# A hybrid backbone on one core: modulation gathered by 32x32 block transposes, tokens loaded first, bias rows without a second buffer

## The chip, the cores and the metric

The kernel runs on one core of one Trainium2 chip. The metric is device time in microseconds (us). The core has a matrix engine (TensorE, PE in the profile), a vector engine (VectorE, DVE), a scalar engine (ScalarE, ACT), a general one (GpSimd, POOL) and a sync engine (SyncE, SP) that here only issues DMA transfers. Each executes its own instructions in order, and the DMA issues of one queue go out in order as well. On chip, tiles lie over 128 partitions; a "128x1024" tile has 1024 numbers in each.

## The reference

256 latent tokens and 256 context tokens of width 2048 pass through two layers. All data are fp32. Layer 0 mixes with a gated DeltaNet (bidirectional, in chunks of 64 tokens) beside neighbourhood attention, layer 1 with a short convolution, and each layer ends in a SwiGLU network with 5632 hidden units. Every layer is modulated by six rows (shift, scale and gate, twice) that are products of one conditioning vector with a 2048 x 12288 matrix. In short:

```python
def modulate(x, g, shift, scale):
    return rmsnorm(x, g) * (1 + scale[..., None, :]) + shift[..., None, :]

for l in range(DEPTH):                                     # DEPTH = 2
    sh1, sc1, g1, sh2, sc2, g2 = split(silu(c) @ ada_w[l] + ada_b[l], 6)
    h = modulate(x_lat, norm_mix[l], sh1, sc1)
    if l % 2 == 0:
        csh1, csc1, ... = split(silu(c_ctx) @ ada_w[l] + ada_b[l], 6)
        hc = modulate(x_ctx, norm_mix[l], csh1, csc1)
        y = even_mixer(h, hc, ...)     # [DeltaNet * silu(za) | attention] @ w_out
    else:
        y = shortconv_mixer(h, ...)
    x_lat = x_lat + g1 * y
    x_lat = x_lat + g2 * swiglu(modulate(x_lat, norm_ffn[l], sh2, sc2), ...)
return rmsnorm(x_lat, final_norm)
```

In the DeltaNet each chunk needs the inverse of a unit triangular 64x64 matrix. In the attention each head adds to its scores a bias from a table of 15 x 31 numbers and a banded mask over the columns of the token grid.

## The kernel before

Nearly all time goes into products of the tokens with large fp32 weights. A weight tile of 128x1024 is loaded raw (512 KB, one issue on the SP queue, L229); ScalarE copies its high part into `whi` (L172), VectorE subtracts to get the low part `wlo` (L243), and PE adds three products for each output tile: high by high, high by low, low by high. `tm_stream` (L274 to L304; matmuls L291, L292, L294) gives outputs with tokens on partitions, `fm_stream` (L306 to L325; matmuls L317 and L321) outputs with features on partitions. Each stream is a Python generator; `drive` advances it one weight tile at a time and runs other work between. The written order is the program's wish. A scheduler with a model of the engines' times then sets the order on each engine and queue, so code that is moved by one step can come out many instructions away.

The start: the modulation of the first mixer is computed eight blocks at a time. `start_block(b)` (L524) loads 4 MB of `ada_w` in four tiles `araw0` (each of two DMAs) and multiplies them with the conditioning vectors (L533, 16 matmuls of 512 columns). `start_tokens(b, ...)` (L537) copies the sums to `mrow` (L540), picks columns by eight matmuls (L546), forms shift and scale, transposes two 128-wide pieces of the normalised tokens `xn` (L191) and writes the modulated tiles `modt` and their high and low parts (L560 to L562). `token_stats` (L565) loads the 4 MB of `xn` (L569), sums squares on ScalarE (L573), takes the root, scales `xn` on VectorE (L576), and is called once, behind `start_block(0)`. The first two streams (`s0`, `s1`) run beside blocks 1 to 7.

Later modulation: for layer 0's remaining parts `ada_mixer` keeps a running sum with one VectorE instruction per half tile (L389) beside the streams and closes a block with four column sums (L396). `ada_job` (L335 to L364) serves layer 1 and the last gate of layer 0: seven jobs of two blocks each. A block adds 16 products (L346) of 128x1024 into `acc`, and then the 128 partitions must be added up and the 1024 sums turned into eight columns of 128. Three of the jobs are of kind "row" (their result goes to DRAM), four of kind "sh" or "sc" (shift and scale).

The middle: after the context's part come the projections QB (two streams of 16 steps), then KB, VB, KB, VB. `plan` calls the inverses (`inverses`, L939) when the count of steps reaches the numbers of `P_INV`: two for the context, then two for the latents. An inverse multiplies by the diagonal blocks `xd` and `xdT`, which SP loads before it; L962, L969 and L975 are its products, and its first product stands behind the latest stream matmul (`issue_after(last_mm[0])`). Then `scan` (L982) and the latents' recurrence follow in pieces between the streams ZA and w_out.

Attention runs head by head with one head ahead: `na_scores` (L1172) loads the head's bias rows `br` (two DMAs, one buffer), its keys `kb` and queries `qb`, adds the band into `bq` (L1183), and takes scores and softmax; `na_values` (L1199) does the rest. The gate `za` is computed by a `tm_stream` whose `za_evac` (L1215) applies silu, multiplies by the norm's gain and stores 128x512 to DRAM on the SP queue (L1220). Its staging tile `zst` has two buffers (`NST`). Then w_out's weights come through a pool of six raw buffers.

## Time and profile before

| | us |
|---|---|
| median of 3 runs | 2819.64 |
| lowest and highest | 2818.58, 2827.38 |
| the profiled execution's own time | 2823.79 |
| its span in the trace | 2822.0 |
| mean granted clock | 0.989 |
| PE busy | 2719.8 (96%) |
| DVE busy | 1920.1 (68%) |
| ACT busy | 1301.9 (46%) |

The span runs from the first recorded instruction to the last, and 1.8 us of the execution's own time lie outside it. A busy PE is the union of matmuls in flight. The granted clock is a share of PE's full speed, so a stretch with 0.86 ran part of the time at the lower of the two levels.

### The profile page before, as it was taken

The page shows a single profiled execution, that of the slowest core. Times are in us where ns is not written, and L with a number is a line of the kernel's source. Part 1 is how long each engine was busy: PE and PEld are TensorE (multiplying, and loading weights), DVE is VectorE, ACT ScalarE, POOL GpSimd, SP SyncE. Part 2 cuts the span into 40 slices and gives each one's busy share as a digit, 9 for nine tenths or more (in the row PEclk, how much of TensorE's full clock was granted, in tenths as well). Part 3 has the DMA queues.
Part 4 walks back from the last instruction along what each step waited for, and adds up shares of the span by engine and source line. Part 5 has one row for each costly group of instructions (what it writes and reads, how often), then busy time and mean ns, then how long its engine had stood idle before and what let it go on. Part 6 is the DMA issues. An engine that isn't in the chain of part 4 may idle for free.

```text
span 2822.0 us, 40405 instructions
## 1 busy us (share of the span) xinstructions
PE 2719.8 (96%) x15113; PEld 2277.5 (81%) x15113; DVE 1920.1 (68%) x2647; ACT 1301.9 (46%) x1943; POOL 50.3 (2%) x77
## 2 busy tenths in 40 slices
PE   5999989999999999999999999999999999999998
PEld 3799989887778788888888878878878888888886
DVE  2377768866767888776678667797678644445665
ACT  2267534322454544444455555444454444444554
POOL 0000100000000000000000000000000000000000
PEclk9999999999999999999999999999999999999999
DMA  9945578887758699987788647998559766656663
GB/s 342 325 135 157 148 234 259 270 250 226 213 200 285 208 333 340 345 291 255 264 283 286 197 154 275 333 327 286 186 196 326 247 193 186 187 188 215 190 192 126
DMA packets 286399, 680.78 MB, mean 241 GB/s; under 512 B 57209, under 2 KB 100833, under 8 KB 284795
## 3 DMA queue, kind: packets, MB, share of 16 engines
q1 hardware_dynamic: 281828, 668.73, 71.3%
q10 hardware_dynamic: 4375, 9.48, 0.9%
q8 instruction: 118, 1.93, 0.3%
q14 instruction: 78, 0.64, 0.1%
HBM read 657.63 MB, written 20.48 MB: 240 GB/s over the span
## 4 chain that ended last, share of the span: by engine, by line
PE 78%; DMA 10%; DVE 6%; ACT 3%; issue 2%; SPq 1%; DVEq 0%; POOL 0%; ACTq 0%
PE mm L294 19%; PE mm L291 19%; PE mm L292 19%; PE mm L321 7%; DMA araw<-in_ada_w_dram 5%; PE mm L300 2%; PE mm L301 2%; PE mm L302 2%; DVE wlo L243 2%; PE sm L191 2%; DMA raw<-in_od_w_in_dram 1%; PE sm L533 1%; DVE acc L346 1%; DVE acc L389 1%; PE gd L321 1%
## 5 line engine op out<-in xcount | busy, mean ns | idle before, releaser
L243 DVE TENSOR_TENSOR wlo<-raw,whi 128x1024 fp32r<-128x1024 f32 x800 | 971.1, 1222 | 436.8 <-ACT whi L172 430.9
L172 ACT ACTIVATE whi<-raw 128x1024 fp32r<-128x1024 f32 x800 | 842.2, 1059 | 825.6 <-PE mm L294 618.9
L292 PE MATMUL mm<-wlo,fhi 128*128 128x512 f32 x1232 | 472.4, 392 | 0.0
L291 PE MATMUL mm<-whi,fhi 128*128 128x512 f32 x1232 | 470.7, 396 | 0.0
L294 PE MATMUL mm<-whi,flo 128*128 128x512 f32 x1232 | 392.2, 392 | 0.1
L346 DVE SCALAR_TENSOR_TENSOR acc<-araw,cT,acc 128x1024 f32<-128x1024 f32 x224 | 287.3, 1283 | 130.2 <-DMA araw<-in_ada_w_dram 123.5
L294 PEld LDWEIGHTS mm<-whi,flo 128*128 128x128 f32 x1232 | 230.8, 188 | 51.1 <-DVE flo L1288 0.5
L292 PEld LDWEIGHTS mm<-wlo,fhi 128*128 128x128 f32 x1232 | 231.8, 188 | 48.7
L291 PEld LDWEIGHTS mm<-whi,fhi 128*128 128x128 f32 x1232 | 231.9, 188 | 48.2
L291 PE MATMUL mm<-whi,ahi 128*128 128x512 f32 x672 | 259.8, 392 | 0.0
L292 PE MATMUL mm<-wlo,ahi 128*128 128x512 f32 x672 | 259.3, 391 | 0.0
L294 PE MATMUL mm<-whi,alo 128*128 128x512 f32 x672 | 209.8, 392 | 0.0
L321 PE MATMUL mm<-hllo,whi 128*128 128x256 f32 x608 | 172.9, 289 | 0.0
L321 PE MATMUL mm<-hlhi,whi 128*128 128x256 f32 x570 | 161.7, 292 | 2.2 <-DVE hlhi L561 1.9
L175 ACT ACTIVATE ahi<-prodT 128x256 fp32r<-128x256 f32 x176 | 73.2, 417 | 194.6 <-PE mm L292 183.9
L389 DVE SCALAR_TENSOR_TENSOR acc<-araw,cT,acc 128x512 f32<-128x512 f32 x192 | 142.7, 747 | 29.1 <-DMA araw<-in_ada_w_dram 27.3
L321 PE MATMUL mm<-hlhi,wlo 128*128 128x256 f32 x570 | 157.8, 289 | 0.0
L292 PEld LDWEIGHTS mm<-wlo,ahi 128*128 128x128 f32 x672 | 126.2, 188 | 27.7
L294 PEld LDWEIGHTS mm<-whi,alo 128*128 128x128 f32 x672 | 126.1, 188 | 27.3
L291 PEld LDWEIGHTS mm<-whi,ahi 128*128 128x128 f32 x672 | 126.2, 188 | 27.1
L292 PE MATMUL mm<-wlo,dhi 128*128 128x512 f32 x336 | 126.4, 396 | 2.2 <-DVE wlo L243 2.2
L291 PE MATMUL mm<-whi,dhi 128*128 128x512 f32 x336 | 123.8, 397 | 0.6 <-DVE u_t L1428 0.6
(419 smaller groups left out, 4194.0 us busy)
## 6 DMA issues: line engine op xcount, KB each, us to landing
araw<-in_ada_w_dram SPq DMA_DIRECT2D x288, 512.0 KB
raw<-in_ffn_w_down_dram SPq DMA_DIRECT2D x176, 512.0 KB
raw<-in_ffn_w_gate_dram SPq DMA_DIRECT2D x160, 512.0 KB
raw<-in_ffn_w_up_dram SPq DMA_DIRECT2D x160, 512.0 KB
raw<-in_ev_w_in_dram SPq DMA_DIRECT2D x112, 512.0 KB
araw<-in_ada_w_dram SPq DMA_DIRECT2D x192, 256.0 KB
raw<-in_od_w_in_dram SPq DMA_DIRECT2D x96, 512.0 KB
raw<-in_ev_w_out_dram SPq DMA_DIRECT2D x32, 512.0 KB
```

What stands on the lines that cost most here:

```text
L172: ACT.activation(dst, src, AF.Copy)
L175: ACT.activation(hi, src, AF.Copy)
L191: return PE.transpose(dst, src, ident[:n, :n])
L243: last_lo[0] = DVE.tensor_tensor(lo, raw, hi, op=OP.subtract).ins
L291: PE.matmul(ps[ti][n], a, hi[:, n * 512:(n + 1) * 512], start=first, stop=False)
L292: PE.matmul(ps[ti][n], a, lo[:, n * 512:(n + 1) * 512], start=False, stop=False)
L294: last_mm[0] = PE.matmul(ps[ti][n], b, hi[:, n * 512:(n + 1) * 512], start=False, stop=False).ins
L300: PE.matmul(ps[ti][n], lh(t), hi[:, c_], start=False, stop=False)
L301: PE.matmul(ps[ti][n], lh(t), lo[:, c_], start=False, stop=False)
L321: last_mm[0] = PE.matmul(ps[f][:, n * 256:(n + 1) * 256], wt, mv(w, k), start=False, stop=i == len(ks) - 1 and g == len(group) - 1 and j = ...
L346: DVE.scalar_tensor_tensor(acc, raw, cT[:, k:k + 1], acc, op0=OP.mult, op1=OP.add)
L389: DVE.scalar_tensor_tensor(accs[n], raws.pop(i), cT[:, k:k + 1], accs[n], op0=OP.mult, op1=OP.add)
```

## The change

Five things change. First, in `ada_job` the gather of a block is replaced by `sum_parts`: VectorE transposes `acc` in blocks of 32x32 (128x1024 in one instruction), adds up each group of 32 (to 128x32), and four fp32 matmuls with the 128x32 constant `fold` add the four groups of partitions. Their result has features on partitions, so "sh" and "sc" jobs take it as it is, and "row" jobs copy it, transpose it once (8 rows of 128) and go on as before. The split of `acc` (ACT and VectorE), 16 selection matmuls, and for "sh" and "sc" a copy and a transpose go away. Second, `token_stats()` is called ahead of `start_block(0)`. Third, the bias rows are loaded straight into `bq`, which has three buffers now, and the band is added in place; `br` is gone. Fourth, the gate store goes out on GpSimd's queue. Fifth, `P_INV` counts differ.

```diff
-P_INV = (30, 32, 79, 80)
+P_INV = (32, 34, 81, 82)
...
+    def sum_parts(dst, pool_, acc, n, tag, bufs):
+        at = pool_.tile([128, 4 * n, 32], F32, name="accT", tag=tag, bufs=bufs)
+        ar = pool_.tile([128, n, 4], F32, name="accR", tag="accR", bufs=bufs)
+        DVE.transpose(at.rearrange("p b r -> p (b r)"), acc)
+        DVE.tensor_reduce(ar.rearrange("p k b -> p (k b)"), at, axis=AX.X, op=OP.add)
+        for b in range(4):
+            PE.matmul(dst[b * 32:b * 32 + 32, 0:n], C("fold"), ar[:, :, b], start=True, stop=True)
...
-            split(ah, al, acc, DVE)
-            for f in range(8):
-                for a in (ah, al):
-                    PE.matmul(p[0:8, 0:128], pick[:, 7 - f:15 - f], a[:, f * 128:(f + 1) * 128],
-                              start=f == 0 and a is ah, stop=f == 7 and a is al)
-            g = pool_.tile([16, 128], F32, name="grow", tag="grow", bufs=1)[0:8]
-            acopy(g, p[0:8, 0:128])
+            sum_parts(p, pool_, acc, 8, "accT", 1)
             if kind == "row":
+                gc = pool_.tile([128, 8], F32, name="gcol8", tag="gcol8", bufs=1)
+                acopy(gc, p[:, 0:8])
+                pc = smt()
+                transpose(pc[0:8, 0:128], gc)
+                g = pool_.tile([16, 128], F32, name="grow", tag="grow", bufs=1)[0:8]
+                acopy(g, pc[0:8, 0:128])
                 ACT.dma_start(row_d[l, seg][fs_], g)
                 continue
-            pc = smt()
-            transpose(pc[:, 0:8], g)
-            ada_done(l, seg, kind, gamma, fs_, pc[:, 0:8])
+            ada_done(l, seg, kind, gamma, fs_, p[:, 0:8])
...
+    token_stats()
     sums = start_block(0)
-    token_stats()
...
-        bq = nap.tile([128, 6, 64], F32, name="bq", tag="bq", bufs=2)
-        br = nap.tile([128, 6, 64], F32, name="br", tag="br", bufs=1)
+        bq = nap.tile([128, 6, 64], F32, name="bq", tag="bq", bufs=3)
...
-            SP.dma_start(br[half * 64:half * 64 + 64], src)
+            SP.dma_start(bq[half * 64:half * 64 + 64], src)
...
-        DVE.tensor_tensor(bq, br, bandf[:, None, :].to_broadcast([128, 6, 64]), op=OP.add)
+        DVE.tensor_tensor(bq, bq, bandf[:, None, :].to_broadcast([128, 6, 64]), op=OP.add)
...
-        SP.dma_start(zd[:, ti, n * 512:(n + 1) * 512], o)
+        POOL.dma_start(zd[:, ti, n * 512:(n + 1) * 512], o)
```

Added lines shift the numbers behind them by 5 or 6: L962, L969 and L975 become L968, L975 and L981, L396 becomes L402, L1180 becomes L1185, and L1220 becomes L1225.

PE's order at the first inverse, before. `mm` are the sums of the QB stream (L321, with `hlhi` and `hllo` the latents' high and low parts), `gd` those of the inverse, and L396 sums a modulation block of layer 0:

```order
L321 MATMUL mm<-hllo,whi 128x256
L321 MATMUL mm<-hlhi,wlo 128x256
L962 MATMUL gd<-xd,n_3970 32x32 x32
L396 MATMUL sm<-cs,acc 128x1 x4
L969 MATMUL gd<-xdT,Y 32x32 x32
L975 MATMUL gd<-Y,xdT 32x32 x32
L321 MATMUL mm<-hlhi,whi 128x256
L321 MATMUL mm<-hllo,whi 128x256
L321 MATMUL mm<-hlhi,whi 128x256
```

The same place in the changed program, where L317 with `h_100` is the first matmul of the KB stream:

```order
L321 MATMUL mm<-hllo,whi 128x256
L321 MATMUL mm<-hlhi,wlo 128x256
L968 MATMUL gd<-xd,n_3970 32x32 x32
L317 MATMUL mm<-h_100,whi 128x512
L321 MATMUL mm<-hllo,whi 128x256
L321 MATMUL mm<-hclo,whi 128x256
L321 MATMUL mm<-h_100,wlo 128x256 x2
L317 MATMUL mm<-h_100,whi 128x512
L321 MATMUL mm<-hllo,whi 128x256
```

The inverse's first product now stands behind the last matmul of QB, with no other work between; the column sums (L402 now) stand 24 rows of QB's matmuls earlier, and L975 and L981, the inverse's next products, follow 22 rows after the first one, among KB's matmuls.

SP's queue where the first attention heads load, before (`vb_d` and `nst` are the last value stores of VB, `kb`, `qb` and `vb` a head's loads):

```order
L1142 DMA vb_d<-nst 128x512 x2
L1180 DMA br<-in_ev_rpb_dram 64x6x64 x2
L1181 DMA kb<-kb_d 128x512
L1142 DMA vb_d<-nst 128x512
L1182 DMA qb<-qb_d 128x256
L1181 DMA kb<-kb_d 128x512
L1182 DMA qb<-qb_d 128x256
L1202 DMA vb<-vb_d 128x4x128
L1180 DMA br<-in_ev_rpb_dram 64x6x64 x2
L1202 DMA vb<-vb_d 128x4x128
```

And in the changed program:

```order
L1148 DMA vb_d<-nst 128x512 x3
L1185 DMA bq<-in_ev_rpb_dram 64x6x64 x2
L1148 DMA vb_d<-nst 128x512
L1186 DMA kb<-kb_d 128x512
L1187 DMA qb<-qb_d 128x256
L1185 DMA bq<-in_ev_rpb_dram 64x6x64 x2
L1186 DMA kb<-kb_d 128x512
L1187 DMA qb<-qb_d 128x256
L1207 DMA vb<-vb_d 128x4x128
L1185 DMA bq<-in_ev_rpb_dram 64x6x64 x2
L1207 DMA vb<-vb_d 128x4x128
```

The second head's bias rows stand right behind the first head's keys and queries, where before the first head's loads and the second's keys stood between, and the third head's rows come one place earlier.

SP's queue at the gate stores, before:

```order
L1220 DMA zd<-zst 128x512 x2
L1202 DMA vb<-vb_d 128x4x128
L1220 DMA zd<-zst 128x512
L229 DMA raw<-in_ev_w_out_dram 128x1024 x2
L1181 DMA kb<-kb_d 128x512
L1182 DMA qb<-qb_d 128x256
L229 DMA raw<-in_ev_w_out_dram 128x1024
```

And in the changed program, where `raw` are the weights of w_out and `araw` those of the modulation:

```order
L1185 DMA bq<-in_ev_rpb_dram 64x6x64 x2
L390 DMA araw<-in_ada_w_dram 128x512 x2
L229 DMA raw<-in_ev_w_out_dram 128x1024 x6
L1207 DMA vb<-vb_d 128x4x128
L229 DMA raw<-in_ev_w_out_dram 128x1024
L390 DMA araw<-in_ada_w_dram 128x512
```

Six weight tiles now stand in a row and no store `zd` is on this queue. The four stores stand on GpSimd's queue, one behind the other, with only fills of `acc` around them.

## Rows read from the trace of the kernel before

**Rows 1.** The line of busy time by engine (first part of the page): busy us, share of the span, instructions.

```profile
PE 2719.8 (96%) x15113; PEld 2277.5 (81%) x15113; DVE 1920.1 (68%) x2647; ACT 1301.9 (46%) x1943; POOL 50.3 (2%) x77
```

**Rows 2.** Table of busy time by stretch: the stretch, its length, then busy us and instructions of PE, PEld, DVE, ACT and POOL, the granted clock, the DMA share, and GB/s. The first two rows are the start and the first weight stream, then come five stretches round two inverses, the bias rows and the gate store, the latents, and all that follows.

```profile
0.00:45.40 45.40, 17.31 (x68) 5.15 (x68) 13.41 (x29) 17.91 (x22) 1.74 (x7) 1.00 0.96 336
45.40:150.00 104.60, 102.74 (x818) 78.19 (x815) 34.80 (x91) 22.74 (x36) 0.00 (x0) 1.00 0.95 305
404.00:428.00 24.00, 20.66 (x351) 20.07 (x349) 12.39 (x18) 8.67 (x14) 0.52 (x1) 0.86 0.83 225
600.00:624.00 24.00, 17.93 (x307) 15.61 (x306) 13.56 (x20) 5.57 (x10) 0.00 (x0) 0.86 0.87 299
684.00:708.00 24.00, 18.23 (x73) 13.06 (x72) 12.33 (x18) 6.02 (x10) 0.00 (x0) 0.86 0.74 207
770.00:780.00 10.00, 6.99 (x51) 6.42 (x49) 7.98 (x18) 6.51 (x12) 0.00 (x0) 1.00 0.87 232
806.00:840.00 34.00, 27.88 (x158) 22.74 (x157) 20.45 (x66) 19.07 (x68) 0.21 (x1) 0.90 0.15 48
924.00:2810.00 1886.00, 1868.13 (x8440) 1529.13 (x8440) 1296.70 (x1440) 899.65 (x1151) 13.94 (x16) 1.00 0.73 245
```

**Rows 3.** The chain of waits in the first 46 us: start, length, what held the chain.

```profile
16.99 13.91 DMA xn<-in_ctx_dram
...
41.86 3.64 PE sm L533 x16
```

**Rows 4.** Timeline of the start, three engines together in this order: the last eight conditioning products of block 0 and its selection matmuls (PE), the scaling of the tokens and the low parts of three weight tiles (DVE), the third high part and the four modulated tiles (ACT), the first stream matmuls, and the first half of block 1's products (PE). Columns: start, length, engine, line, operation, count, and in brackets the idle time before and what ended it.

```profile
21.26 1.94 PE L533 MATMUL sm<-araw,cT 128*32 128x512 f32 x8 [1.15 <-DMA araw<-in_ada_w_dram]
...
24.00 1.87 PE L546 MATMUL sm<-cs,mrow 128*128 128x2 f32 x8 [0.80 <-DVE mrow L540]
...
35.34 4.87 DVE L576 TENSOR_SCALAR xn<-xn,n0r 128x2048 f32<-128x2048 f32 x4
...
40.13 3.49 DVE L243 TENSOR_TENSOR wlo<-raw,whi 128x1024 fp32r<-128x1024 f32 x3
...
38.13 1.06 ACT L172 ACTIVATE whi<-raw 128x1024 fp32r<-128x1024 f32 x1 [0.29 <-DMA raw<-in_ev_w_in_dram]
...
40.78 1.93 ACT L560 ACTIVATE modt<-sm,sh,sc 128x256 f32<-128x256 f32 x4 [1.59 <-PE sm L191]
...
45.43 2.08 PE L317 MATMUL mm<-h,whi 128*128 128x512 f32 x4
...
49.73 1.06 PE L533 MATMUL sm<-araw,cT 128*32 128x512 f32 x8
```

**Rows 5.** What the gather costs today, and the nearest rows to what replaces it: one of the 16 selection matmuls of a block and the stream matmul behind them (timeline), 64 small fp32 records of an inverse and the eight records of four column sums of layer 0 (timeline, 0.75 and 1.02 us from first start to last end), the vector engine's low part of the accumulator and its 32x32 transpose of 32x128 (by line and form: min/median/max ns), and a stretch in which a gather falls (columns as in the table by stretch).

```profile
1028.86 0.22 PE L355 MATMUL sm<-ah,pick 128*8 128x128 f32 x1
...
1029.82 0.45 PE L292 MATMUL mm<-wlo,fhi 128*128 128x512 f32 x1
...
415.26 0.75 PE L962 MATMUL gd<-xd,n 32*32 32x32 f32 x64
...
415.98 1.02 PE L396 MATMUL sm<-cs,acc 128*128 128x1 f32 x8
...
L176 DVE TENSOR_TENSOR al<-acc,ah x14: 1214/1224/1226, 1018.5 to 2311.1; 128x1024 fp32r<-128x1024 f32 x14
...
L880 DVE STREAM_TRANSPOSE dgs<-nt x32: 292/302/309, 223.3 to 501.5; 32x128 f32<-32x128 f32 x32
...
1850.00:1910.00 60.00, 57.07 (x272) 45.35 (x270) 53.40 (x64) 27.09 (x36) 0.96 (x1) 1.00 0.95 345
```

**Rows 6.** The first bias rows: the DMA issue of the second head's rows (SPq is the sync engine's queue), the addition that waits for them, and the two matmuls that stand behind it (timeline).

```profile
686.62 1.27 SPq L1180 DMA_DIRECT2D br<-in_ev_rpb_dram  x2
...
696.13 0.56 DVE L1183 TENSOR_TENSOR bq<-br,cs 128x384 f32<-128x384 f32 x1 [5.74 <-DMA br<-in_ev_rpb_dram]
...
697.88 0.50 PE L292 MATMUL mm<-wlo,hlhi 128*128 128x512 f32 x1 [2.27 <-DVE wlo L243]
...
701.60 2.08 PE L838 MATMUL gd<-cs,gm 128*128 128x128 f32 x8 [2.99 <-DVE AT L1074]
```

**Rows 7.** The gate stores: two issues on the sync queue, then one, then the first two weight tiles of w_out; the first matmul that needs such a tile (timeline); and, by line and form, the vector engine's tensor_scalar of 128x512.

```profile
760.08 1.69 SPq L1220 DMA_DIRECT2D zd<-zst  x2
...
769.51 0.32 SPq L1220 DMA_DIRECT2D zd<-zst  x1
...
769.88 0.92 SPq L229 DMA_DIRECT2D raw<-in_ev_w_out_dram  x2
...
776.41 1.20 PE L291 MATMUL mm<-whi,yhi 128*128 128x512 f32 x4 [3.01 <-ACT whi L172]
...
L1196 DVE TENSOR_SCALAR s<-s,l x16: 435/480/488, 709.0 to 831.8; 128x512 f32<-128x512 f32 x16
```

**Rows 8.** At the first inverse: the four raw weight issues after the loads of the diagonal blocks, and the scalar engine's first high part from them (timeline); and the modulation sums of layer 0 (costliest groups of the page: count, busy us, mean ns, idle before).

```profile
415.20 2.21 SPq L229 DMA_DIRECT2D raw<-in_ev_w_in_dram  x4
...
420.81 1.06 ACT L172 ACTIVATE whi<-raw 128x1024 fp32r<-128x1024 f32 x1 [4.37 <-DMA raw<-in_ev_w_in_dram]
...
L389 DVE SCALAR_TENSOR_TENSOR acc<-araw,cT,acc 128x512 f32<-128x512 f32 x192 | 142.7, 747 | 29.1 <-DMA araw<-in_ada_w_dram 27.3
```

**Rows 9.** The third inverse's first 64x64 product, and a value product at the end of the latents' chain (timeline of PE).

```profile
616.29 0.44 PE L962 MATMUL gd<-xd,n 64*64 64x64 f32 x2 [4.13 <-DVE xd L977]
...
830.66 3.78 PE L1211 MATMUL gd<-PT,vb 128*128 128x256 f32 x8 [3.66 <-ACT PT L167]
```

2 lines of the change are left out of this document (removed).

## The prediction

> **What bounds the kernel now.** I read the busy times by engine first: PE is busy 96% of the span [rows 1], so time comes back only where PE does less, waits less or runs at a higher clock. The table by stretch shows where that can be. From 924 us on PE is idle 17.9 of 1886 us and the clock is full [rows 2], so two thirds of the run have almost no waits to remove. The idle time sits in the start (28.1 of 45.4 us), at the two inverses (3.3 us of 404 to 428, 6.1 us of 600 to 624), at the first bias rows (5.8 us of 684 to 708), at w_out's first weights (3.0 us of 770 to 780) and in the latents (6.1 us of 806 to 840) [rows 2]. [...] A stretch at 0.86 does 24 x 0.14 = 3.4 us less work than at 1.00. So a wait is worth its idle time and, where it takes the clock down, up to 3.4 us on top. Then I read the chain of waits at the start and the timelines at the places that the change touches.
>
> **The start.** The chain runs through the tokens' DMA, which holds it from 16.99 for 13.91 us, and ends in L533 x16 of 3.64 us [rows 3]. Behind the last tokens stand the scaling on DVE (35.34 to 40.21), three low parts (40.13 to 43.62), the four modulated tiles on ACT, and the first stream matmul at 45.43 [rows 4]. In the changed program the same 8.4 MB (tokens and block 0) go out in the other order. The DMA engines are 0.96 busy over the start [rows 2], so the last byte still lands at about 30.9 (16.99 + 13.91). But what lands last is then block 0, and the tokens' sums, root and scaling are done in its shadow. Behind it stand: the last eight of L533 1.94, `mrow` 0.7 to 0.8 (L546's idle before it), L546 1.87 [rows 4], shift and scale (three short operations, for which I allow 0.6), and two of the low parts (1.2 each) that DVE takes before them. That puts the modulated tiles at about 30.9 + 1.9 + 0.8 + 1.9 + 0.6 + 1.2 = 37.3 or earlier, against 40.78, and the first stream matmul 3.5 us or so before 45.43. What is late next is the weights: from 45 to 150 us the DMA share is 0.95 at 305 GB/s [rows 2], and a part of the gain can be lost again to a later block's data. L533 of block 1 (two halves of 1.06 at full speed, against 3.64 for 16 at the start) moves behind the stream's start in place of standing ahead of it. I take -3.5, from -6 (all of that and a cheaper L533) to -1.
>
> **The gather.** PE's 16 selection matmuls take 0.96 us a block (1028.86 to 1029.82), and there are 14 blocks, as the 14 low parts show [rows 5]: 13.4 us, beside nothing, since PE is the bound there. Four fp32 fold matmuls come in their place, each recorded as two: eight records. The nearest rows are 64 records in 0.75 us with weights of 32 columns and eight in 1.02 us with weights of 128 [rows 5], so 0.09 to 1.02 a block. The fold has a weight of 128x32 and eight columns out; its loads have all partitions as L396's do, and I take 0.70. That is (0.70 - 0.96) x 14 = -3.6. For "row" blocks a transpose is added, for the others one goes: nothing. ACT loses a copy of 1024 columns a block and was not waited for. DVE loses `al` (1.22) and gains a transpose and a reduction of the same 1024 numbers, which no row shows at this size: between 1.22 each (the row of `al`, same length) and 2.4 (eight times the transpose of 128 numbers, 302 ns). I take 1.24 each, near the row of the same length, so +1.26 us a block on DVE. From 924 us on DVE is busy 1296.7 of 1886 us [rows 2], which hides it. The cover is thin at one place, 1850 to 1910, where DVE is busy 53.4 of 60 and PE already idle 2.9 [rows 5]: two blocks, half a microsecond each, +1 (0 to +5, at 2.4 each). Sum -2.6.
>
> The row of `al` has 1224 ns for 1024 numbers, and the transpose's 302 ns for 128 is more than an eighth of it [rows 5]. [...]
>
> **Bias rows.** DVE, in order, waits 5.74 us at 696.13 for `br`; the issue of such rows is at 686.62, since the single buffer comes free only with the addition of the head before [rows 6]. Behind the waiting addition stand the low part and the mask product, and PE waits 2.27 us at 697.88 and 2.99 us at 701.60 for them [rows 6]; with the clock (0.86) the place costs 5.3 + 3.4 = 8.6 us. With three buffers SP can issue the rows two heads ahead, and the second head's stand behind the first head's keys. The adding itself stays at 0.56. What is late next is the weights' high part and the latents' scores; the clock need not come back whole. I take -6 (0 to -8.6).
>
> **w_out's first weights.** The sync queue issues two gate stores at 760.08 and one at 769.51, each of which must wait for `za_evac`, and the first two raw tiles of w_out stand behind it at 769.88; PE waits 3.01 us at 776.41 for the high part [rows 7]. Off this queue, the tiles go out as their buffers come free. I take -2 (0 to -3).
>
> **First inverse.** SP's issues of the KB weights at 415.20 come behind the loads of the diagonal blocks, and the high part waits 4.37 us for them and starts at 420.81 [rows 8]. PE fills 0.75 + 1.02 us of that with L962 and L396, and something over a microsecond with L969 and L975, standing idle 3.3 us. In the changed order L402 stands 24 rows ahead and L975 and L981 22 rows behind: the weights' wait is filled by L968 alone, so about 1.2 us more idle, and DVE must do five modulation sums (0.75 each [rows 8]) before the copies of `xd` where it had one. I take +3 (-2 to +6).
>
> **Third inverse.** PE waits 4.13 us at 616.29 for `xd` from DVE [rows 9]. The new step number moves the call by two steps, the chain through DVE is the same, and nothing in the order takes the sums out of its way: 0 (-9.4, if the 6.1 idle and the 3.4 of clock both go, to +5).
>
> **Latents' end.** The last recurrence has stream work to hide behind: before its first state product some 105 matmuls of ZA and 51 of w_out are left, in the changed order 43 and 51. At 1868.13/8440 = 0.22 us a record [rows 2] that is 14 us less cover. The tail, 806 to 840, has 6.1 us idle and a clock of 0.90, with waits like the 3.66 us at 830.66 for ACT [rows 2, 9]. I take +1.5 (0 to +8), since the chain also starts earlier by what the bias rows and w_out give.
>
> **Sum.** -3.5 - 2.6 - 6 - 2 + 3 + 0 + 1.5 = -9.6 us, against the profiled execution's 2823.79 (a span of 2822.0 and 1.8 around it): 2814.2. That execution lies 4.2 above the median of 2819.64; medians are compared, so I take the difference from there: 2810.0.
>
> **The rivals.**
> Smaller gain: the DMA queue, 0.95 busy until 150 us, takes back the start's 3.5, and the first inverse costs its upper 6: 2810 + 3.5 + 3 = 2816.5. For it: no block's bytes become fewer. Against it: the tokens' work does leave the chain.
> Faster: the third inverse meets its `xd` in time because two more steps of stream lie ahead of it: 2810 - 9.4 = 2800.6. Against it: the wait is on DVE's queue, which moves with it.
> Slower, by one mechanism: the latents' recurrence runs out of cover. If the 14 us that left are uncovered in full, and the clock falls twice at 3.4, the place costs 20.8 in place of 1.5: 2829.3. It decides from about 11 us of uncovered chain on, where the whole gain is used up. For it: the tail has idle time already. Against it: most of the recurrence waits on itself while PE does attention, not only streams.
> The gather waits: the folds stand in PE's order right behind a chain of two DVE operations (2.5 us); if 0.8 us of that shows in each of 14 blocks, 2810 + 11.2 = 2821.2.
> Stores late on GpSimd: `zst` has two buffers, and between the pair and the third store lie 9.4 us [rows 7]; a store would have to be some 8 us late for the evacuation to wait. Then about +4: 2814. DVE is busy with tensor_scalar work of 480 ns beside them [rows 7]. [...]
>
> **How the numbers follow.** Forecast 0.50 (own range 2803 to 2817), smaller gain 0.25, faster 0.10, latents 0.08, the gather waits 0.04, stores late 0.03. 0.3% is 8.5 us, which is about what a measurement of this kernel can tell from no change: faster is under 2811.2, slower over 2828.1. Faster: two thirds of the forecast (0.33), all of the faster case, a quarter of the smaller gain, a little of the last: 0.50. Slower: most of the latents' case and the tails of the others, 0.08. The rest, 0.42, is within. The range 2798 to 2822 leaves out the latents' case and the outer edges of the others.
>
> **What would show it.** Right: first L317 at 41 to 43 us; eight fold records within 0.7 us of each other; no wait for the bias rows at 690 to 705 and a clock near 1.00 there; w_out's high part without the 3 us wait; DVE transposes near 1.2 us. Wrong: the stream's gain gone by 150 us, PE idle in front of the folds, a longer idle time in the latents' tail, or waits at the first or third inverse other than told.

## The result and the profile after

The changed kernel takes 2837.34 us (median of 6 runs, 2835.21 to 2839.90) against 2825.08 for the kernel before (6 runs, 2818.58 to 2828.20): a ratio of 1.0047, 95% interval 1.0035 to 1.0059. It is slower by 12 to 13 us, where the forecast was 10 us faster. (The forecast started from 2819.64, the median of the first three runs; three more put it at 2825.08.) The profiled execution took 2837.88 us, its span is 2836.1.

The line of busy time by engine, which answers to [rows 1]:

```profile
PE 2720.1 (96%) x14999; PEld 2268.8 (80%) x14999; DVE 1934.5 (68%) x2661; ACT 1284.1 (45%) x1924; POOL 58.2 (2%) x81
```

PE is busy for the same 2720 us in a span that is 14 us longer, though 114 matmuls fewer are recorded. The table by stretch, same stretches and columns as [rows 2]:

```profile
0.00:45.40 45.40, 19.27 (x85) 9.71 (x86) 13.35 (x29) 17.79 (x22) 0.73 (x5) 1.00 0.96 326
45.40:150.00 104.60, 100.02 (x777) 72.23 (x777) 32.71 (x82) 21.10 (x33) 0.99 (x2) 0.98 0.97 309
404.00:428.00 24.00, 16.38 (x128) 16.30 (x128) 9.99 (x12) 6.89 (x7) 0.52 (x1) 0.86 0.82 223
600.00:624.00 24.00, 21.86 (x161) 20.48 (x159) 12.22 (x19) 4.10 (x5) 2.41 (x3) 1.00 0.76 190
684.00:708.00 24.00, 21.59 (x103) 16.59 (x102) 19.26 (x30) 7.72 (x14) 0.00 (x0) 1.00 0.92 277
770.00:780.00 10.00, 6.99 (x28) 5.88 (x29) 7.89 (x13) 8.73 (x20) 1.08 (x2) 0.69 0.49 169
806.00:840.00 34.00, 29.22 (x187) 24.04 (x185) 17.87 (x54) 16.95 (x72) 0.00 (x0) 1.00 0.15 48
924.00:2810.00 1886.00, 1863.82 (x8320) 1517.92 (x8319) 1311.82 (x1454) 886.27 (x1135) 13.94 (x16) 0.99 0.73 247
```

Some places look as the forecast wanted them: PE idle 2.4 us in 684 to 708 (5.8 before) and 2.1 in 600 to 624 (6.1), with the clock at 1.00 in both where it was 0.86. (The second stretch no longer holds the third inverse, which has moved behind it, as the rows below show.) Others are worse: 404 to 428 has 7.6 us idle (3.3 before), and 770 to 780 has the clock at 0.69. Time per stretch doesn't yet tell what a wait is worth; fixed points of the program do. The timelines of PE have these points at the following times (starts of instructions, ends where it says so; "value product" is the attention's L1211, L1216 after; the first down projection is counted up to the first matmul of the next product, the last one from the end of the matmul before it):

| | before | after |
|---|---|---|
| first stream matmul (L317) | 45.4 | 38.9 |
| eighth block's selection matmuls (L546, L552) | 146.5 | 149.0 |
| QB's last first-tile matmul (L317), then KB's first | 400.6, 428.1 | 402.5, 431.8 |
| latents' first state product | 719.2 | 738.2 |
| end of the ZA stream | 768.5 | 759.3 |
| last value product | 837.0 | 849.1 |
| end of w_out | 922.3 | 934.3 |
| first down projection, length | 254.0 | 256.5 |
| last down projection, length | 242.6 | 246.3 |
| end of the last stream | 2808.3 | 2822.1 |

PE's rows of the start, which answer to [rows 4] (the first conditioning products, which by the row now follow the tokens' statistics, the first stream matmul, the eighth selection), and the wait for weights that stood beside the first inverse ([rows 8]) and now stands bare (the matmul that waits is one of QB's last, so these are QB's weights and not yet KB's, as I had read them):

```profile
23.01 1.94 PE L539 MATMUL sm<-araw,cT 128*32 128x512 f32 x8 [10.78 <-DVE n0s L219]
...
38.94 2.08 PE L317 MATMUL mm<-h,whi 128*128 128x512 f32 x4 [0.57 <-DVE h L567]
...
149.04 0.50 PE L552 MATMUL sm<-cs,mrow 128*128 128x2 f32 x4
```

```profile
425.48 0.58 PE L321 MATMUL mm<-hlhi,whi 128*128 128x256 f32 x1 [7.62 <-ACT whi L172]
```

The start is 6.5 us ahead at 39 and 2.5 behind at 149. The ZA stream ends 9.2 us earlier, and yet w_out ends 12 later. From the last value product to the end of w_out it is 85 us in both. So this product, and the chain that leads to it, sets the end of the middle, and not the ZA stream beside it. It is 12.1 of the 14.1 us. The rest lies behind: the down projections are 2.5 and 3.7 us longer, although no line of theirs was changed, and the other stretches behind w_out, where the gathers fall, are about 4 us shorter.

PE's timeline of the chain, before and then after: the first product of the latents' first inverse (the third inverse), the latents' first state product and the last value product:

```profile
602.00 0.75 PE L962 MATMUL gd<-xd,n 32*32 32x32 f32 x64
...
719.19 1.05 PE L1000 MATMUL gd<-state,kT 128*128 128x128 f32 x8
...
836.98 1.97 PE L1211 MATMUL sm<-PT,vb 128*128 128x256 f32 x8 [0.31 <-issue]
```

```profile
628.99 0.75 PE L968 MATMUL gd<-xd,n 32*32 32x32 f32 x64
...
738.24 1.05 PE L1006 MATMUL gd<-state,kT 128*128 128x128 f32 x8
...
849.10 1.97 PE L1216 MATMUL sm<-PT,vb 128*128 128x256 f32 x8 [0.39 <-issue]
```

The third inverse starts 27 us late, the recurrence 19 us, and its end is 12 us late. Between start and end of the recurrence stands another wait. Timelines of the changed kernel round the gate stores, in the order of their causes: SP's issue of the six w_out tiles, the vector engine's addition of bias rows, the first three gate stores on GpSimd, the scalar engine's third gate evacuation, the vector engine behind it, and PE behind that:

```profile
752.79 8.51 SPq L229 DMA_DIRECT2D raw<-in_ev_w_out_dram  x6
...
758.67 0.56 DVE L1188 TENSOR_TENSOR bq<-bq,cs 128x384 f32<-128x384 f32 x1 [4.59 <-DMA bq<-in_ev_rpb_dram]
...
761.17 0.67 POOL L1225 DMA_DIRECT2D zd<-zst  x1 [88.84 <-DVE zst L1224]
...
762.97 0.54 POOL L1225 DMA_DIRECT2D zd<-zst  x1 [1.13 <-DVE zst L1224]
...
772.21 0.54 POOL L1225 DMA_DIRECT2D zd<-zst  x1 [8.70 <-DVE zst L1224]
...
770.60 0.60 ACT L1222 ACTIVATE zst<-mm 128x512 f32<-128x512 f32 x1 [13.38 <-DMA zd<-zst]
...
771.23 0.69 DVE L1224 TENSOR_TENSOR zst<-zst,gnb 128x512 f32<-128x512 f32 x1 [8.57 <-ACT zst L1222]
...
773.01 2.08 PE L1026 MATMUL gd<-R,xdT 128*128 128x128 f32 x8 [7.32 <-DVE R L1009]
```

Three megabytes of weights go out from 752.79 on. The first evacuations were done by 757, but the gain's multiplication on DVE stands behind the addition, which waits 4.59 us for its rows; so the stores start at 761. Then the first of them needs until 770.5 to land, `zst` has two buffers, and ACT waits 13.38 us, DVE 8.57 and PE 7.32. PE's wait of 3.01 us for w_out's weights [rows 7] is gone; this one is for `R`, a tile of the recurrence.

The list of DMA issues gives the median time from issue to landing (last column, us), for the first two stores and then for the other two, ahead of which no weights had been issued for 11 us:

```profile
zd<-zst POOLq DMA_DIRECT2D x2, 256.0 KB, 9.0
...
zd<-zst POOLq DMA_DIRECT2D x2, 256.0 KB, 2.4
```

The same queue thus took 9.0 us with six weight tiles issued ahead of it and 2.4 without them.

### The profile page after: what moved, and what is told of

Read it like the earlier page. It is cut to its first block, busy times and chain, and to the rows that moved or that the text cites. A ratio compares the mean times of both kernels' runs of the same rounds, so it can differ in the third digit from the quotient of the medians.

```text
span 2836.1 us, 40147 instructions
## 1 busy us (share of the span) xinstructions
PE 2720.1 (96%) x14999; PEld 2268.8 (80%) x14999; DVE 1934.5 (68%) x2661; ACT 1284.1 (45%) x1924; POOL 58.2 (2%) x81
## 5 line engine op out<-in xcount | busy, mean ns | idle before, releaser
L172 ACT ACTIVATE whi<-raw 128x1024 fp32r<-128x1024 f32 x800 | 842.9, 1059 | 907.0 <-PE mm L294 627.5
L321 PE MATMUL mm<-hllo,whi 128*128 128x256 f32 x608 | 173.0, 289 | 0.0
L321 PE MATMUL mm<-hlhi,whi 128*128 128x256 f32 x570 | 161.8, 292 | 10.6 <-ACT whi L172 7.6
L321 PE MATMUL mm<-hlhi,wlo 128*128 128x256 f32 x570 | 159.2, 290 | 0.0
L176 DVE TENSOR_TENSOR alo<-prodT,ahi 128x256 fp32r<-128x256 f32 x176 | 74.3, 424 | 85.5 <-PE mm L294 80.0
```

The costliest lines, as they stand in the source:

```text
L172: ACT.activation(dst, src, AF.Copy)
L176: (eng or DVE).tensor_tensor(lo, src, hi, op=OP.subtract)
L321: last_mm[0] = PE.matmul(ps[f][:, n * 256:(n + 1) * 256], wt, mv(w, k), start=False, stop=i == len(ks) - 1 and g == len(group) - 1 and j = ...
```

## The experiments

Two theories were put up first. **A, the late recurrence:** the inverses called two steps later start the recurrence 19 us later, and its end is passed on. **B, the gate stores:** the wait of 13.38 us is passed on. Times are medians; ratios are to the kernel before as it was timed beside each run, with their 95% interval.

**Undoing the step numbers, the gate store's queue, both, or giving a third buffer.** All four start from the changed kernel:

```diff
-P_INV = (32, 34, 81, 82)          # first and third run
+P_INV = (30, 32, 79, 80)
...
-        POOL.dma_start(zd[:, ti, n * 512:(n + 1) * 512], o)     # second and third
+        SP.dma_start(zd[:, ti, n * 512:(n + 1) * 512], o)
...
-NST = 2                            # fourth
+NST = 3
```

> The changed kernel with the old step numbers for the inverses. Its trace has the latents' first state product at 738.2 us (before: 719.2) and the recurrence's last value product at 849.1 (before: 837.0). Theory A (late latents: the inverses called two steps later start the recurrence 19 us later, and its end sets the end of w_out): the first state product comes back to about 719, and the time falls by 10 to 14 us, to 2823 to 2828. Theory B (gate stores: the scalar engine waits 13.4 us at 770.6 for gate stores that stand behind six weight tiles): the recurrence starts earlier but still meets the same wait of the scalar engine, and the time falls by at most 5 us, to 2832 or more.

> The changed kernel with the gate store back on the sync queue. Theory A: the recurrence still starts near 738 us and the time stays within 3 us of 2837. Theory B: the 13.4 us wait of the scalar engine and the 7.3 us wait of PE at 773 go, a wait of about 3 us for w_out's first weights returns, and the time falls by 6 to 12 us, to 2825 to 2831.

> The changed kernel with both undone, so that only the start, the gather and the bias rows differ from the kernel before. If A and B together are the whole loss, 2816 to 2823, 2 to 9 us under the kernel before, since PE saves about 3 us in the gather and the bias rows' waits are gone. If something else in the change costs time (the start's other order, the folds), 2828 or more.

> The changed kernel with three staging buffers in place of two, the gate store still on GpSimd's queue. Theory B by the buffer (the store is late, and the third evacuation waits for its buffer): the scalar engine's wait at the third evacuation goes or shrinks below 4 us, the time falls as in the run with the store on the sync queue, to 2825 to 2831. Theory A: within 3 us of 2837. If the lateness holds up others than the evacuation (the weights themselves late), the time stays too, but the scalar engine's wait is gone.

| run | time, us | ratio | first state product | last value product | longest wait for a store on ACT |
|---|---|---|---|---|---|
| changed | 2837.3 | 1.0047 (1.0035 to 1.0059) | 738.2 | 849.1 | 13.4 |
| old numbers | 2826.6 | 1.0006 (0.9995 to 1.0017) | 713.7 | 835.5 | 6.5 |
| store on SP | 2830.9 | 1.0025 (1.0015 to 1.0035) | 740.4 | 843.8 | 5.2 |
| both | 2824.1 | 1.0003 (0.9990 to 1.0015) | 716.7 | 839.3 | 6.4 |
| third buffer | 2828.0 | 1.0012 (1.0001 to 1.0023) | 729.3 | 841.0 | 12.0 |

A came out as expected: with the old numbers alone the recurrence starts 24 us earlier and 11 us are back. (The run puts the context's two numbers back as well.) B did too, with 6 us from the other queue: the recurrence starts 2 us later still, but from its first state product to the last value product it needs 103.4 us in place of 110.9. They don't add up: both together bring no more than the numbers alone. With the old numbers the first two stores go out at 762.8 and 763.5, ahead of the first weight tile at 764.6, so the other queue has little left to gain. The scalar engine's row with the old numbers, and with the third buffer, where the fourth evacuation now waits in the third's place:

```profile
765.36 0.60 ACT L1222 ACTIVATE zst<-mm 128x512 f32<-128x512 f32 x1 [6.47 <-DMA zd<-zst]
```

```profile
761.72 0.60 ACT L1222 ACTIVATE zst<-mm 128x512 f32<-128x512 f32 x1 [11.99 <-DMA zd<-zst]
```

The third buffer moves the wait to the next evacuation; its gain came from elsewhere: the staging buffers serve the QB, KB and VB stores too, and the middle ran 8 us ahead before any gate store (last VB matmul 669.8 against 677.8). The wait of some 6 us that is left with the old numbers is on whichever queue (6.5 and 6.4); the kernel before has none at this place, and the bias rows alone, below, bring one of 5.9. The run with both undone fell short of its expectation (2816 to 2823): the start, the gather and the bias rows together gain nothing.

**Each gaining part alone, and the dose of A.** These start from the kernel before; the first three add one part of the change's diff each, the fourth is

```diff
-P_INV = (30, 32, 79, 80)
+P_INV = (30, 32, 77, 78)
```

and a fifth has 75 and 76.

> The kernel before with the tokens loaded ahead, alone. The forecast's own term was -3.5 us. In the changed kernel the first stream matmul came 6.5 us earlier, but the eighth block's selection matmuls at 149.0 against 146.5. If the DMA engines, busy 0.98 until then, set the end of the start, the gain is gone at 147 to 150 us and the time stays within 3 us of the kernel before; the first stream matmul is still near 39. If the forecast's term holds, the eighth block's selection comes at 143 and the time is 3 to 4 us lower.

> The kernel before with the new gather, alone. Forecast: -2.6 us. The changed kernel shows eight fold records within 0.25 us against 0.96 for the selection, which would be -10 us in 14 blocks if nothing came back. In all five profiles with the new gather the last down projection takes 246.3 us against 242.6 before. If that belongs to the gather's tiles (where they put the others), it is 246.3 here too, and the whole is -4 to -8. If it belongs to the chip or to the other edits, 242.6 and -8 to -10.

> The kernel before with the bias rows loaded straight into three buffers, alone. Forecast: -6 us, PE's waits of 2.27 and 2.99 us at 698 and 702 gone and the clock whole there. Rival: the last value product (837.0 in the kernel before, and 85.2 us of w_out after it in every profile so far) is set by the recurrence, and the vector engine's waits for the rows come back with later heads, as in the changed kernel (19.6 us in eight waits, 14.6 in four before): then the last value product stays within 2 us of 837 and the time within 3 us.

> The kernel before with the latents' inverses two steps EARLIER (77, 78 in place of 79, 80), nothing else. Theory A by its dose: two steps later cost 19 us of the recurrence's start and about 12 us of the time; two steps earlier start the recurrence about 15 to 20 us earlier, and the last value product comes earlier by 3 to 10 us if the recurrence sets it: 2814 to 2821. If the attention heads and the streams set it from here on, the last value product stays at 837 and the time at 2823 to 2825, and the old number is already early enough.

> The kernel before with the latents' inverses four steps earlier (75, 76). Theory A continued: the last value product was 837.0 at 79/80, 829.0 at 77/78; another 3 to 8 us earlier, the time 2809 to 2814. If the first state product no longer sets the pace (heads and streams do), it stays at 829 or comes later, and the time at 2815 to 2820.

| run | time, us | ratio | first state product | last value product |
|---|---|---|---|---|
| start alone | 2827.9 | 1.0013 (1.0000 to 1.0025) | 722.4 | 840.8 |
| gather alone | 2820.5 | 0.9994 (0.9982 to 1.0005) | 717.8 | 836.4 |
| bias rows alone | 2826.9 | 1.0010 (0.9998 to 1.0022) | 711.6 | 833.9 |
| 77, 78 | 2816.7 | 0.9972 (0.9962 to 0.9982) | 707.5 | 829.0 |
| 75, 76 | 2818.5 | 0.9987 (0.9975 to 0.9999) | 696.3 | 830.0 |

The dose bears A out, up to a point: two steps earlier than before brings the last value product 8 us forward and the time with it; four steps start the recurrence another 11 us earlier and nothing more follows, so from there something else sets the pace (the expectation names the heads and streams; which it is was not followed up). PE's rows at 77, 78:

```profile
707.52 1.05 PE L1000 MATMUL gd<-state,kT 128*128 128x128 f32 x8
...
828.98 1.97 PE L1211 MATMUL sm<-PT,vb 128*128 128x256 f32 x8 [0.39 <-issue]
```

With the start alone the first stream matmul comes at 38.9 and the eighth selection at 149.9, 3 us later than before. The bytes ahead of that selection are the same: 322 GB/s up to 146.5 us before and 317 up to 149.0 in the changed kernel are both 47.2 MB, at a DMA share of 0.98 and 0.97. So the time of the start is that of its transfers, and the new order does not move them faster. Table by stretch (columns as in [rows 2], DMA share and GB/s last), before, then the changed kernel, then one stretch of the changed kernel with the old numbers, which has the same start:

```profile
10.00:20.00 10.00, 4.50 (x18) 0.79 (x18) 0.66 (x3) 1.71 (x3) 0.00 (x0) 1.00 0.94 311
110.00:120.00 10.00, 10.00 (x86) 8.45 (x79) 2.23 (x8) 1.81 (x3) 0.00 (x0) 1.00 1.04 335
```

```profile
10.00:20.00 10.00, 0.68 (x2) 0.36 (x2) 0.60 (x3) 8.03 (x10) 0.00 (x0) 1.00 0.85 309
110.00:120.00 10.00, 10.00 (x83) 6.56 (x73) 0.84 (x3) 0.00 (x0) 0.00 (x0) 0.97 0.85 275
```

```profile
110.00:120.00 10.00, 10.00 (x84) 8.05 (x83) 2.23 (x8) 1.46 (x3) 0.00 (x0) 1.00 1.07 344
```

At 10 to 20 us the share falls from 0.94 to 0.85, but the bytes do not (309 against 311 GB/s). At 110 to 120 us 275 GB/s go for 335: 0.6 MB less, which is 1.8 us at the higher rate. Without this gap (third table) the eighth selection comes at 146.8, so the start's gain is gone even there. Over all profiles it comes at 145.3 to 146.5 us with the old start and at 146.8 to 150.7 with the new one. What makes the gap was not tried. In the time the loss is at the edge of the interval (1.0000 to 1.0025).

With the bias rows alone the vector engine waits no less than before, for later heads (seven waits, 19.6 us together; four and 14.6 before). Two of these waits, and on SP's queue the issue of the keys and that of the rows for the second of them:

```profile
733.30 0.56 DVE L1182 TENSOR_TENSOR bq<-bq,cs 128x384 f32<-128x384 f32 x1 [4.91 <-DMA bq<-in_ev_rpb_dram]
...
756.24 0.56 DVE L1182 TENSOR_TENSOR bq<-bq,cs 128x384 f32<-128x384 f32 x1 [4.36 <-DMA bq<-in_ev_rpb_dram]
...
747.21 0.33 SPq L1180 DMA_DIRECT2D kb<-kb_d  x1
...
748.10 1.27 SPq L1179 DMA_DIRECT2D bq<-in_ev_rpb_dram  x2
```

The rows are still late for the addition, only for other heads. From their issue to the addition it is 8.1 us here and 9.5 in [rows 6]: the issue itself comes late, and here it stands right behind loads of keys and queries. Why the third buffer does not bring it forward was not followed up, and an earlier issue was not tried. The recurrence starts 7.6 us earlier in this profile and the last value product comes 3.1 us earlier, but behind w_out this profile is 6 us longer (1891.9 us from the end of w_out to the last matmul, 1885.9 before), for which the run shows no cause, and the time shows no gain.

**The gather's missing gain.** Its folds cost PE less than forecast, and still the gather alone brought only 3 us, which is within its interval (4 to 8 were expected with the 246.3 us that came). All profiles with the new gather had a last down projection of 246.3 us, all with the old one 242.6, and no gather falls into it. What the gather does change there is where the tiles lie: its pool is smaller, and the pool behind it holds `prodT` and the down projection's stationary tiles. By the built programs `prodT` begins at byte 153088 of each partition before, and at 149184 with the new gather. Two runs gave the pool an unused tile, which no instruction reads or writes: 984 numbers with the new gather (153152), 16 numbers with the old one (153152 too). A third run has the first tile and the earlier inverses, a fourth the first tile in the changed kernel.

```diff
         wr = ada_w[l].rearrange("(k p) n -> p k n", p=128)
+        pool_.tile([128, 984], F32, name="pad", tag="pad", bufs=1)   # 16 with the old gather
         for blk in range(2):
```

> The kernel before with the new gather, and an unused tile of 984 numbers in the gather's pool, so that what is placed behind that pool lies where it lay before. In every profile so far the last down projection takes 242.6 us with the old gather and 246.3 with the new one, and no gather falls in it. If it is where the tiles lie, it is 242.6 here and the whole comes 3 to 5 us under the run of the gather alone (2820.5): 2815 to 2818. If it is something else that the gather brings, 246.3 and no change.

> The same with the latents' inverses two steps earlier (77, 78). If the two gains add up: the earlier inverses alone were 7.9 us under the kernel before (0.9972), so 2808 to 2812, a ratio of 0.994 to 0.996. If they don't (the last value product set by something else than the recurrence), 2814 to 2818.

> The changed kernel with the unused tile of 984 numbers in the gather's pool, nothing else. The gather alone lost 14 us (2820.5 to 2809.5) when this tile was added; with it prodT and the tiles of the down projections behind it lie at 153152 bytes in each partition, without it at 149184, in the kernel before at 153088. If this is a loss of its own beside the late recurrence, the last down projection takes 240.3 us here and the time is 9 to 14 us below 2837: 2823 to 2828, the kernel before again. If it hung on the rest of that kernel, 2834 or more.

> The kernel before with an unused tile of 16 numbers (64 bytes in each partition) in the pool of the old gather: no instruction changes, prodT moves from 153088 to 153152 bytes. If the place alone sets the rate, the down projections take 249.4 and 240.3 us in place of 254.0 and 242.6, and the time is 6 to 7 us under the kernel before, 2816 to 2818. If the rate belongs to the new gather with its other tile, 254.0 and 242.6 stay and the time is the kernel before's.

| run | time, us | ratio | down projections, us |
|---|---|---|---|
| gather alone | 2820.5 | 0.9994 (0.9982 to 1.0005) | 255.7, 246.3 |
| gather, tile | 2809.5 | 0.9951 (0.9934 to 0.9969) | 249.4, 240.3 |
| gather, tile, 77 and 78 | 2806.1 | 0.9941 (0.9926 to 0.9956) | 249.4, 240.3 |
| changed, tile | 2825.2 | 1.0001 (0.9990 to 1.0012) | 249.6, 240.3 |
| before, tile of 16 | 2822.1 | 0.9993 (0.9983 to 1.0003) | 252.7, 240.3 |

One line and form of the last down projection and its busy time (100 us of each; min/median/max ns), for before, after, before with 64 bytes more, and the gather with its tile:

```profile
L292 PE MATMUL mm<-wlo,ahi x139: 388/392/394, 2600.1 to 2699.9; 128*128 128x512 f32 x139
...
2600.00:2700.00 100.00, 100.00 (x438) 82.05 (x438) 66.33 (x86) 56.94 (x83) 0.00 (x0) 1.00 0.59 187
```

```profile
L292 PE MATMUL mm<-wlo,ahi x135: 390/392/404, 2600.5 to 2699.5; 128*128 128x512 f32 x135
...
2600.00:2700.00 100.00, 100.00 (x432) 81.07 (x431) 60.93 (x76) 51.90 (x73) 0.00 (x0) 1.00 0.60 189
```

```profile
L292 PE MATMUL mm<-wlo,ahi x139: 389/389/389, 2600.0 to 2698.8; 128*128 128x512 f32 x139
...
2600.00:2700.00 100.00, 100.00 (x443) 82.81 (x442) 66.10 (x85) 57.30 (x84) 0.00 (x0) 1.00 0.58 187
```

```profile
L292 PE MATMUL mm<-wlo,ahi x139: 389/389/389, 2600.3 to 2699.6; 128*128 128x512 f32 x139
...
2600.00:2700.00 100.00, 100.00 (x443) 82.81 (x442) 67.27 (x86) 57.19 (x84) 0.00 (x0) 1.00 0.60 194
```

The clock reads 1.00 in all of them, and the engine is busy without a gap; yet 438, 432, 443 and 443 matmuls are recorded in the same 100 us. With 64 bytes more, and not one instruction changed, the spread of 388 to 394 ns becomes a steady 389. The place alone sets this rate. Its size for the kernel before was overrated: 6 to 7 us were expected, 3.6 came in the two projections and 2 in the time, which is within the noise. The expected 249.4 us of the first projection were those of the new gather, whose cheaper gathers fall into that projection too. For the changed kernel the place is 12 us. With its tile the gather brings 14 us (6 to 9 were expected: the tile was meant to bring back the old place and 242.6 us, and met a better one). Of these 14 us, 11 stand between the gather with and without the tile. The gain lies where the gathers and the down projections are: from the end of w_out to the last matmul it is 1884 to 1892 us in the profiles with the old gather, 1883 to 1889 with the new one, and 1872 to 1879 with the new one and its tile.

**The store on the scalar engine's queue, and the last combinations.** The first is the changed kernel with `ACT.dma_start` for the store. The second is gather, tile, 77 and 78 with the bias rows on top; the third and fourth are the changed kernel with the tile and the numbers 79, 80 or 77, 78.

> The changed kernel with the gate store on the scalar engine's queue: the six weight tiles of w_out stand in the same row on SP's queue as with GpSimd's. If the stores are late because three megabytes of weights were issued ahead of them and share the same 16 DMA engines, the third evacuation waits 8 us or more here too and the time is within 4 us of 2837. If it is GpSimd's queue (its first packet moves 4 to 5 us after the issue), the wait falls to 5 us or less and the time to 2828 to 2832.

> The new gather with the unused tile, the latents' inverses two steps earlier, and the bias rows loaded straight. The first two gave 2806.1. The bias rows alone brought the last value product 3 us forward and took nothing from the time. If that adds up where the recurrence starts early, 2802 to 2805; if the rows only move the waits, 2805 to 2809.

> The changed kernel with the old step numbers and the unused tile of 984 numbers: its start, gather, bias rows and GpSimd stores stay. Alone the numbers took 11 us off (2826.6) and the tile 12 (2825.2). If the late recurrence and the place are two losses in different parts of the program, they add up: 2811 to 2816, a ratio of 0.996 to 0.998. If one hides the other, 2822 or more.

> The same with the step numbers 77 and 78 for the latents and 30 and 32 for the context. On the kernel before, two steps earlier took 7 to 8 us off, and beside gather and tile 3. If the stores on GpSimd's queue still meet the six weight tiles, the scalar engine waits 5 us or more at the third evacuation and the gain is at most 3: 2809 to 2814. If not, 2804 to 2808.

| run | time, us | ratio | last value product | longest wait for a store on ACT |
|---|---|---|---|---|
| store on ACT | 2837.4 | 1.0046 (1.0031 to 1.0062) | 851.7 | 6.6 |
| gather, tile, 77, bias rows | 2814.1 | 0.9958 (0.9945 to 0.9971) | 836.8 | 4.3 |
| changed, tile, 79 | 2817.3 | 0.9974 (0.9962 to 0.9985) | 842.9 | 6.6 |
| changed, tile, 77 | 2818.0 | 0.9981 (0.9969 to 0.9994) | 840.2 | 11.4 |

With the store on ACT the time is the changed kernel's to the microsecond. Rows of SP, DVE and ACT at the place:

```profile
756.18 18.45 SPq L229 DMA_DIRECT2D raw<-in_ev_w_out_dram  x6
...
762.36 0.56 DVE L1188 TENSOR_TENSOR bq<-bq,cs 128x384 f32<-128x384 f32 x1 [4.92 <-DMA bq<-in_ev_rpb_dram]
...
764.97 0.60 ACT L1222 ACTIVATE zst<-mm 128x512 f32<-128x512 f32 x1 [6.34 <-DVE zst L1224]
...
772.14 0.60 ACT L1222 ACTIVATE zst<-mm 128x512 f32<-128x512 f32 x1 [6.57 <-DMA zd<-zst]
```

The same six tiles stand on SP's queue, five of them issued before the first store at 764.6 (the row's 18.45 us run on to the sixth); the addition waits 4.92 us for bias rows, the second evacuation 6.34 for the vector engine, the third 6.57 for its store. So the lateness doesn't belong to GpSimd's queue: behind 2.5 to 3 MB of weights the first store took 9.3 us to land on that queue, and some 7.5 on the scalar engine's (764.6 to 772.1). (The third evacuation's wait is 6.6 us, under the 8 that were expected, since the second has lost as much already.)

The bias rows on top of gather, tile, 77 and 78 were expected to gain 1 to 4 us over 2806.1 or to change nothing (2802 to 2809). The run came out at 2814.1, with the last value product 4.9 us later (836.8 against 831.9): they gain nothing in this company either, and by the ratios (0.9958 against 0.9941) rather cost some 5 us, which the intervals do not settle.

The last two runs came out at 2817 and 2818 where 2811 to 2816 and 2804 to 2814 were expected. The first misses by less than the intervals of 0.1% can tell, so that the two losses add up is neither shown nor excluded. The second gained nothing over the first: there the stores behind the weights still hold the third evacuation for 11.4 us. The best version is the gather with its tile and the numbers 77 and 78, 0.59% under the kernel before (0.44% to 0.74%); start, bias rows and store are as before in it.

## Why the prediction was wrong

The forecast was -9.6 us, the result is +12.3. The old step numbers alone give 10.7 us back, the unused tile alone 12.1, both together 20.0; the other queue for the gate stores gives 6.4, which overlaps with the numbers. By terms of the sum:

- **Latents' end, +1.5 (0 to +8): the step that failed.** The mechanism was named, and again as the slower rival with 0.08, but priced by cover (14 us of stream less) and not by the start of the chain. I read from the order that the recurrence had fewer matmuls beside it (105 of ZA became 43, as in the trace) and did not ask when it begins. It began 19 us later, its end came 12 us later, and the run with the old numbers gave 11 us back. The idle time already there in the tail [rows 9] was a sign that the chain and not PE's work sets the end; that two steps earlier than before bring another 7 us shows it. From the last value product to the end of w_out it is 85 to 87 us in every profile.
- **Third inverse, 0.** The 4.13 us wait did go, as the faster rival had it, but not because `xd` met an inverse in its old place: the inverse starts 27 us later, at 629.0. Over 600 to 672 us, which hold it in both kernels, PE is idle 3.9 us where it was 6.1, with the clock at 1.00 for 0.95. The same move cost the recurrence its start. I had priced the inverse where it stands and not what waits for it later.
- **Bias rows, -6.** PE's waits at 698 and 702 shrank and the clock came back, as said: 5.8 us idle became 2.4. (The forecast's 3.4 us for the clock, from 24 us at 0.86 [rows 2], agree with the trace: by steps of 1 us the kernel before has 0.83 from 699, 0.50 from 700 to 706 and 0.76 from 706, behind PE's waits, and 1.00 in the rest of the stretch.) The time got nothing from it (1.0010 alone). In the changed kernel the vector engine waits for rows eight times, 19.6 us together, and one of these waits holds up the gate stores. This is the sum's largest gain, and it was counted as if PE's idle time there were on the path; alone it moved the last value product by 3.1 us, and where these went is not shown.
- **w_out's first weights, -2.** The sign was wrong: the wait of 3.01 us for the weights went, and one of 7.32 us for the recurrence came at the same place; the store's queue alone is worth 6 us the other way. The rival on late stores named the place and priced it at +4, with a chance of 0.03. It did not ask for the cause: that weights freed from the wait would go out first. The first store landed 9.3 us after its issue, at a DMA share of 0.94 and 315 GB/s from 761.2 to 770.5. The vector engine's work, which the rival set beside the stores, was not the cause: DVE stood idle for 8.57 us while the first two were out, the later stores of the same queue landed in 2.4 us, and the scalar engine's queue gave the same time.
- **Start, -3.5.** The first stream matmul came at 38.9 (41 to 43 forecast), so more of the tokens' work is hidden behind the loads than I worked out. (My sum for it also holds only one of the two low parts that it names; it came out earlier all the same.) The loads of the next blocks took all of it and 0.3 to 4.2 us more (146.8 to 150.7 against 146.5). "A part can be lost" was the doubt; with the same bytes to move at a DMA share of 0.95 it had to be the forecast.
- **Gather, -2.6.** Right in kind, wrong in size on both sides. A fold holds PE for 0.18 us, not 0.70, as the rows behind this list show, so PE saves 0.78 x 14 = 10.9 us. The vector engine's two operations took 1.245 and 1.210 us, as priced: both are within 2% of the 1.224 of `al`, the row of the same length [rows 5], and the proportional 2.4 us is excluded. PE waits at the folds of two of the 14 blocks, 1.51 us at 1791 for the reduction and 0.67 at 1884 for another tile of the vector engine (`ocv`). The loss by place, 2.5 and 3.7 us in the two down projections, was in no term.
- **First inverse, +3.** Near: the QB stream before it is 1.9 us late, KB's first matmul 3.7, so it cost 1.8; the wait for the weights grew to 7.62 us, and L968, which I had filling it, moved behind it with the last 24 rows of QB.

PE at one fold and the stream matmul behind it; the vector engine's transpose and reduction by line and form (min/median/max ns); and the fold that waited:

```profile
1042.42 0.25 PE L343 MATMUL sm<-accR,cs 128*32 128x8 f32 x8
...
1042.60 0.51 PE L294 MATMUL mm<-whi,flo 128*128 128x512 f32 x1
...
L340 DVE STREAM_TRANSPOSE accT<-acc x14: 1234/1245/1249, 1029.7 to 2221.7; 128x1024 f32<-128x1024 f32 x14
...
L341 DVE TENSOR_REDUCE accR<-accT x14: 1207/1210/1221, 1032.0 to 2305.9; 128x32 f32<-128x1024 f32 x14
...
1791.13 0.25 PE L343 MATMUL sm<-accR,cs 128*32 128x8 f32 x8 [1.51 <-DVE accR L341]
```

## What to carry to other kernels

Before pricing waits, find the point behind which the rest of the program has a constant length, and follow back from there: a wait that doesn't lie on that chain need not be worth anything, and a call moved later is priced by what waits for its result. A transfer that is taken off a queue lets the next ones go first, and can land late behind them (here in 9.0 us in place of 2.4). When a tile is taken out of a pool, compare the stages whose code did not change, and try an unused tile before giving the edit up.

## What was not expected of the hardware

Where the tiles of the down projection lie in the partition changed the rate of its matmuls at full clock: 388 to 394, 390 to 404 or a steady 389 ns for the same instructions. Over the 1056 matmuls of the last down projection that is 242.6, 246.3 or 240.3 us, the same to 0.1 us in every profile of kernels with the same gather and tile (`prodT` at 153088, 149184, 153152). Which of the down projection's tiles it is, and why 64 bytes matter, was not tried and stays open. Open too is whether the late recurrence and the place add up to the full sum when both are taken away, and why the bias rows, which bring the recurrence forward, bring nothing in the time.
